# A two-branch decoder layer: the up product with tokens on the partitions, two of eight K-pairs by seven products

## The chip, the cores and the metric

The kernel runs on one core of one Trainium2 chip. The metric is the device time of one execution in microseconds (us). An interval or a verdict comes from several runs of both kernels on the same chip.

## What is computed

One decoder layer over 256 tokens of width 2048, in float32. An attention branch and an mLSTM branch fill the first part and end in a gated sum and an output projection. The second part is a feed-forward block, and the change is about this block:

```python
h2 = rmsnorm(x, norm2_g[l])
u = causal_dwconv(jnp.einsum('bsd,df->bsf', h2, w_up[l]), conv_w[l], conv_b[l])
u_gate, u_val = u[..., :D_FF], u[..., D_FF:]
x = x + jnp.einsum('bsf,fd->bsd', jax.nn.silu(u_gate) * u_val, w_down[l])
```

`w_up` is 2048 x 11264 and `w_down` 5632 x 2048. The convolution has three taps per channel and runs over the tokens: out[t] = w0 u[t-2] + w1 u[t-1] + w2 u[t] + b. So it wants the channels on the partitions and the tokens along the free dimension.

## The kernel before, in words

**Products in two parts.** Every operand is split into a high part (rounded to the float32r type) and a low part (the rest), and a product is three matmuls: low x high, high x high, high x low. For weights, ScalarE writes the high part `wh` (L159) and VectorE the low part `wl` (L160), piece by piece; a piece is 1024 columns wide. There are three buffers each of `wh` and `wl`, so the split runs at most two pieces ahead of TensorE. Weight chunks (1 MB, two pieces) come by SyncE's queue into three buffers `raw` (L122). `next_sub` (L165) hands TensorE its next piece and writes the split of the pieces after it into the program.

**Two forms of product.** With the tokens on the partitions (`block_b`, L233, and `s_block`, L267), 128 tokens are the stationary operand and 512 weight columns move: a 256 x 256 x 1024 piece of work, called a K-pair here (two K-tiles of 128, two token tiles, two column halves), takes 8 products, 24 matmuls of 512 columns. With the channels on the partitions (`block_a`, L260) the weights are stationary and the activations move: per K-tile one matmul of 512 columns (`wh` against the high and the low activation side by side) and one of 256 (`wl` against the high one).

**Seven products.** In `s_block` a pattern says for each K-pair whether it is done plainly ("p") or by seven products instead of eight ("S"), that is 21 matmuls instead of 24. For an "S" pair the weights need sums: the chunk gives four pieces, "b" (1024 columns), "b21" (512), "t13" (1024) and "t24" (1024). VectorE makes the sums (L144, L151, L154) besides the low parts, and the sum tile for "t24" is finished by L154, which is written with "t13". The activations need sums too (`put_sums`, L204). Such patterns stand in the gate projections, the output projection and the last product (Y_PAIRS, 8 of 22 pairs). TensorE and the vector engines each work through their own list in a fixed order that the compiler's scheduler sets.

**The up product before.** 88 blocks of 128 channels, gate and value in turn (`block_a`, called at L919), 16 K-tiles each. `up_evac` (L897) then adds the two halves of the PSUM tile (ScalarE L350, VectorE L351), multiplies by the row norm (`rb`, VectorE L900), and convolves (ScalarE L903, two VectorE instructions L905). Silu is on ScalarE (L923), the product with the value on VectorE (L926, into `gv`). Every second pair `put_pair` (L200) splits the result into the operand of the last product (`ghl`), and for the 8 "S" pairs of the last product `put_sums` writes sums that go out to DRAM (`s_dram`, L933) and come back after the up product (`s_ops`, L943). The normalisation is applied after the product, so `h2` is the plain sum stream times the gain, transposed (`transposed`, L848).

**Buffers.** A pool "a8" has 15 tiles of 8 KB per partition; the eleven `ghl` tiles and the four `h2` tiles fill it during the up product. Scratch has four 2 KB tiles.

**Elsewhere.** At the start, the squares of x for the first norm are taken on ScalarE from the transposed x and added up on GpSimd (`add_square`, L429). Before the gate projections, `normalised` (L602) loads the transposed x a second time by GpSimd's queue (L600, `hv`), scales it on VectorE (L607) and splits it into `hN`.

Of the kernel before, what the change touches and what calls it, by code (L numbers as in the profile page):

```python
# [17 lines left out]
P = 128  # L18
# [19 lines left out]
WO_PAIRS = "pSpSpppp"  # L38
Y_PAIRS = "ppp" + "Sp" * 7 + "S" + "pppp"
N_S = Y_PAIRS.count("S")  # L40

C_G1, C_G2, C_QG, C_KG, C_MG, C_CONV = 0, 16, 32, 33, 34, 42
CST = C_CONV + 2 * NF * 4


@with_exitstack  # L50
def trunk(ctx: ExitStack, tc: tile.TileContext, a):
# [19 lines left out]
    def scratch(name, shape, tag="w2k", bufs=4):  # L71
        return work.tile(shape, F32, tag=tag, bufs=bufs, name=name)
# [10 lines left out]
    def add_chunk(ap, n, pieces=("whole", "whole")):  # L83

        subs_of.extend((len(chunks), i, kind) for i, kind in enumerate(pieces))
        chunks.append((ap, n, ap.tensor.name))
# [19 lines left out]
    n = len(subs_of)  # L106
# [4 lines left out]
    raws, subs, s_tiles, last_of = {}, {}, {"of": None}, {}  # L111
    n_chunk = len(chunks)

    def load_chunk(i, part=None):
# [3 lines left out]
        src, n, _ = chunks[i]  # L118
# [5 lines left out]
    def split_sub(j):  # L124
# [142 lines left out]
    def s_block(name, pairs, s_ops, pattern, pools, dst, add=True, per_piece=0):  # L267
# [22 lines left out]
        for m, kind in enumerate(pattern):  # L290
# [18 lines left out]
            left -= 1  # L309
            if first:  # L310
                ps = {i: pools[1](f"{name}p{i}") for i in (1, 5, 7, 6)}
            s1, s2, s3, s4 = s_ops[m]
            w = piece()
# [46 lines left out]
    hT, _ = operand("hT")  # L360
# [64 lines left out]
    sq = const.tile([P, S], F32, name="sq")  # L425
# [3 lines left out]
    def add_square(x, first):  # L429

        if first:
            nc.scalar.activation(sq, x, AF.Square)
            return
        t = scratch("t2", [P, S], tag="u1k", bufs=5)
        nc.scalar.activation(t, x, AF.Square)
        nc.gpsimd.tensor_tensor(sq, sq, t, ALU.add)

    def norm(r):

        ps = aux_tile("ps_norm")  # L440
        for tok in range(2):
            mm(ps[:, tok : tok + 1], sq[:, tok * P : (tok + 1) * P], ones[:, :1], True, True)
        v = small("v", [P, 2], 1)
# [595 lines left out]
```

## Time and profile before

| what | value |
|---|---|
| median of 3 runs | 1399.7 us (1393.97 to 1401.78) |
| the profiled execution's own time | 1392.95 us |
| its span, first to last instruction | 1391.2 us |
| granted TensorE clock, mean | 0.999 |
| TensorE busy | 1378.4 us of the span |
| VectorE busy | 1056.4 us |
| ScalarE busy | 762.1 us |
| GpSimd busy | 49.7 us |
| matmuls of the up product | 1408 of 512 columns, 1408 of 256 |

How to read the profile: its page gives the busy time of each engine, the span in 40 slices, and the chain of work that ended last, followed back from the last instruction. PE is TensorE (PEld its weight loads), DVE VectorE, ACT ScalarE, POOL GpSimd, SP SyncE. Matmuls overlap in the pipeline, so the duration of one is longer than the distance from one start to the next; it is this distance that adds up to the time of a stage. The timeline shows it: start, length, instruction, and in brackets the idle time before it with what ended it. The same holds for VectorE: two independent instructions in a row overlap a little. L numbers are lines of the kernel before; rows of the changed kernel's order have that kernel's own lines (there the low part of a weight piece is L173, the sums L157, L164 and L167).

### The profile page before, as it was taken

The numbers are of one execution on the slowest core, as the hardware profiler recorded it, in microseconds if no ns is written. First come the engines' busy times: TensorE is split into PE (matmuls) and PEld (weight loads), VectorE is DVE, ScalarE is ACT, GpSimd is POOL, SyncE is SP. The second block draws the span as 40 slices with busy tenths as digits, with TensorE's granted clock in tenths as the row PEclk, the third lists the DMA queues.
The fourth block names the chain that finished last, engine by engine and source line by source line (L and its number), as shares of the span: only waits on it lengthen the run. The fifth ranks groups of instructions, "written<-read, shape, count | busy, mean of one in ns | idle before, by whom it ended". The sixth has DMA issues, their size and how long they took to land.

```text
span 1391.2 us, 18429 instructions
## 1 busy us (share of the span) xinstructions
PE 1378.4 (99%) x6956; PEld 1165.0 (84%) x6956; DVE 1056.4 (76%) x1493; ACT 762.1 (55%) x1086; POOL 49.7 (4%) x84
## 2 busy tenths in 40 slices
PE   8999999999999999999999999999999999999998
PEld 8978788888788888887888888888888888878877
DVE  7565566556888867777888888888888887886886
ACT  6645454444655544454755565656565554653553
POOL 6001100000000000000000000000000000000000
PEclk9999999999999999999999999999999999999999
DMA  7645564443555566465555556555555657657553
GB/s 253 213 180 182 197 227 156 168 161 122 181 193 221 191 229 220 160 229 217 186 191 201 194 195 207 191 199 199 208 203 182 231 201 266 220 185 270 205 188 121
DMA packets 43128, 276.25 MB, mean 199 GB/s; under 512 B 4960, under 2 KB 4976, under 8 KB 12192
## 3 DMA queue, kind: packets, MB, share of 16 engines
q1 hardware_dynamic: 39168, 260.20, 52.6%
q0 software_dynamic: 3728, 14.87, 3.0%
q8 instruction: 54, 0.88, 0.3%
q14 instruction: 34, 0.28, 0.1%
q10 hardware_dynamic: 144, 0.02, 0.0%
HBM read 267.73 MB, written 7.34 MB: 198 GB/s over the span
## 4 chain that ended last, share of the span: by engine, by line
PE 96%; DVE 2%; DMA 1%; ACT 0%; issue 0%; POOL 0%; ACTq 0%; DVEq 0%
PE up L220 35%; PE y0q L220 7%; PE y1q L220 7%; PE p L220 6%; PE mog L220 3%; PE fq L220 3%; PE mv L220 3%; PE fk L220 3%; PE wo0q L220 3%; PE wo1q L220 3%; PE g1q L220 2%; PE g3q L220 2%; PE g2q L220 2%; PE g0q L220 2%; PE fv L220 2%; PE y0p L220 2%
## 5 line engine op out<-in xcount | busy, mean ns | idle before, releaser
L159 ACT ACTIVATE wh<-raw 128x1024 fp32r<-128x1024 f32 (+2 forms) x496 | 505.8, 1021 | 473.9 <-PE up L220 120.3
L160 DVE TENSOR_TENSOR wl<-raw,wh 128x1024 fp32r<-128x1024 f32 (+2 forms) x496 | 580.3, 1182 | 200.4 <-ACT wh L159 198.2
L220 PE MATMUL up<-h,wh 128*128 128x512 f32 x1408 | 488.6, 391 | 0.0
L220 PE MATMUL up<-h,wl 128*128 128x256 f32 x1408 | 394.0, 280 | 0.0
L220 PEld LDWEIGHTS up<-h,wh 128*128 128x128 f32 x1408 | 263.2, 187 | 58.0 <-DVE h L189 0.2
L220 PEld LDWEIGHTS up<-h,wl 128*128 128x128 f32 x1408 | 266.1, 189 | 0.1
L160 DVE TENSOR_TENSOR wl<-sums,wh 128x1024 fp32r<-128x1024 f32 x58 | 70.9, 1223 | 46.6 <-ACT wh L159 46.6
L159 ACT ACTIVATE wh<-sums 128x1024 fp32r<-128x1024 f32 x58 | 61.5, 1060 | 67.1 <-PE y0q L220 19.4
L905 DVE SCALAR_TENSOR_TENSOR t<-u,cst,t 128x256 f32<-128x256 f32 x176 | 84.8, 482 | 3.8 <-ACT t L903 0.7
L220 PE MATMUL p<-wh,am 128*128 128x512 f32 x256 | 79.4, 391 | 0.0
L220 PE MATMUL y1q<-wh,ghl 128*128 128x512 f32 x256 | 78.1, 390 | 0.0
L220 PE MATMUL y0q<-wh,ghl 128*128 128x512 f32 x256 | 78.0, 390 | 0.0
L220 PEld LDWEIGHTS y1q<-wh,ghl 128*128 128x128 f32 x256 | 48.1, 188 | 10.1
L220 PEld LDWEIGHTS y0q<-wh,ghl 128*128 128x128 f32 x256 | 48.0, 188 | 10.1
L220 PEld LDWEIGHTS p<-wh,am 128*128 128x128 f32 x256 | 47.6, 188 | 9.7
L903 ACT ACTIVATE t<-u,cst 128x256 f32<-128x256 f32 x88 | 52.0, 591 | 1.8 <-DVE u L900 1.6
L220 PE MATMUL p<-wl,am 128*128 128x512 f32 x128 | 49.9, 390 | 0.0
L220 PE MATMUL y0q<-wl,ghl 128*128 128x512 f32 x128 | 48.9, 391 | 0.0
L220 PE MATMUL y1q<-wl,ghl 128*128 128x512 f32 x128 | 48.8, 390 | 0.0
L220 PE MATMUL mog<-wh,hT 128*128 128x348 f32 (+1 forms) x192 | 43.5, 337 | 2.4 <-ACT wh L159 1.9
L220 PE MATMUL g0q<-wh,hN 128*128 128x512 f32 x128 | 41.5, 404 | 0.0
L220 PE MATMUL mv<-wh,hT 128*128 128x512 f32 x128 | 40.2, 395 | 0.0
(372 smaller groups left out, 2032.0 us busy)
## 6 DMA issues: line engine op xcount, KB each, us to landing
raw<-in_w_up SPq DMA_DIRECT2D x88, 1024.0 KB, 4.9
raw<-in_w_dn SPq DMA_DIRECT2D x44, 1024.0 KB, 4.8
raw<-in_w_g SPq DMA_DIRECT2D x32, 1024.0 KB, 4.9
raw<-in_w_fox SPq DMA_DIRECT2D x24, 1024.0 KB, 4.8
raw<-in_w_p SPq DMA_DIRECT2D x16, 1024.0 KB, 4.9
raw<-in_w_out SPq DMA_DIRECT2D x16, 1024.0 KB, 4.9
raw<-in_w_mqk SPq DMA_DIRECT2D x8, 1024.0 KB, 4.8
raw<-in_w_mv SPq DMA_DIRECT2D x8, 1024.0 KB, 4.8
```

The lines of the kernel that those rows point to most:

```text
L159: nc.scalar.activation(wh[:, :n], src, AF.Copy)
L160: nc.vector.tensor_tensor(wl[:, :n], src, wh[:, :n].bitcast(F32), ALU.subtract)
L220: nc.tensor.matmul(out, lhsT, rhs, start=start, stop=stop)
L903: nc.scalar.activation(t, u[:, 2:], AF.Identity, scale=w[2], bias=w[3])
L905: nc.vector.scalar_tensor_tensor(out=t, in0=u[:, i : i + S], scalar=w[i], in1=t, op0=ALU.mult, op1=ALU.add)
```

## The change

The up product is done by `s_block`, tokens on the partitions, in 11 blocks of 1024 columns (512 gate, 512 value channels), each of eight K-pairs with the pattern "ppSpSppp". Its result `c` is token-major. VectorE adds the plain part to the seven-product part (four instructions of 512), ScalarE scales by a per-token factor `rho`. Then, during the next block, `as_columns` transposes it back on TensorE (four transposes of 128 columns for each of 44 channel groups), ScalarE copies it out of PSUM, and `convolved` does the convolution, Silu and the splits as before. A list of tasks says where: four empty tasks, then one transpose group, and so on, two tasks per weight piece, so that all of it falls into the first eight pieces of the twenty of a block. The row norm becomes: `x2` is scaled by `rs`, the norm of its first half, before it is transposed, and `rho` corrects to the full norm. The order of the K-pairs in the last product is rotated by six; the six pairs 0 to 5 are written to DRAM (`g_dram`) and read back (`gback`) before it, and the sums' scratch moves from the "mv" tile to the 2 KB scratch.

At the start the squares are taken from x in token-major form (`xt`, two loads of 1 MB by GpSimd's queue), eight ScalarE instructions of 512 with their own accumulator, and GpSimd's sums go. `normalised` rebuilds the operand from the split one already in SBUF (`whole`, one add, one multiply, one split) instead of loading x again.

The core of the diff:

```diff
+UP_PAIRS = "ppSpSppp"
+N_OUT = 6
+Y_ORDER = list(range(N_OUT, NF // 2)) + list(range(N_OUT))
...
-    add_b(a["w_up"], 512)
-    subs_of[n + 1], subs_of[n + 2] = subs_of[n + 2], subs_of[n + 1]
+    add_pairs(a["w_up"], [UP_PAIRS] * (NF // 4))
...
-        add_square(xT[k], k == 0)
+        if k == 2:
+            for tok in range(2):
+                nc.gpsimd.dma_start(xt[tok], a["x"][tok * P : (tok + 1) * P, :])
+        if k >= KD // 2:
+            tok, q = divmod(k - KD // 2, 4)
+            add_squares(ss1[:, tok, q : q + 1], xt[tok][:, q * 512 : (q + 1) * 512])
...
+    def whole(pair):
+        v = scratch("gv", [P, 2, S])
+        nc.vector.tensor_tensor(
+            v, pair[:, :, 0, :].bitcast(F32), pair[:, :, 1, :].bitcast(F32), ALU.add
+        )
+        return v
     def normalised(m):
-        load_x(m + 1)
-        v = hv.pop(m)
...
+        v = whole(hT_pairs[m])
+        nc.vector.tensor_tensor(v, v, rb.unsqueeze(1).to_broadcast([P, 2, S]), ALU.mult)
         put_pair(hN_pairs[m], v.rearrange("p k s -> p (k s)"))
...
+    def as_columns(j, c):
+        ps, at = (aux_tile if j // 4 % 2 == 0 else acc_tile)(f"ps_u{j}"), j % 4 * P
+        for h in range(2):
+            for tok in range(2):
+                nc.tensor.transpose(
+                    ps[:, h * S + tok * P : h * S + (tok + 1) * P],
+                    c[:, tok, h * 512 + at : h * 512 + at + P], ident,
+                )
+        us[j] = work.tile([P, 2, S], F32, tag="u2k", bufs=2, name=f"u{j}")
+        nc.scalar.activation(us[j].rearrange("p h s -> p (h s)"), ps, AF.Copy)
+    def convolved(j):
+        u, out = us.pop(j), []
+        for i in range(2):
...
+            nc.scalar.activation(t, u[:, i, :], AF.Identity, scale=w[2], bias=w[3])
+            for q in (1, 0):
+                d = 2 - q
+                nc.vector.scalar_tensor_tensor(
+                    out=t[:, d:], in0=u[:, i, : S - d], scalar=w[q], in1=t[:, d:], op0=ALU.mult,
+                    op1=ALU.add,
+                )
...
+        nc.vector.tensor_tensor(gv[:, (j % 2) * S : (j % 2 + 1) * S], sg, out[1], ALU.mult)
...
+            put_sums(gv, se, False)
...
+        put_pair(g_pairs[m], gv)
+        if m < N_OUT:
+            nc.gpsimd.dma_start(
+                g_dram[:, m], g_pairs[m].rearrange("p k l s -> p (k l s)")
+            )
...
+    for b in range(NF // 4):
+        pools = (aux_tile, acc_tile) if b % 2 == 0 else (acc_tile, aux_tile)
+        c = a8(f"c{b}", [2, 1024])
...
+        q = s_block(f"up{b}", h2_pairs, up_ops, UP_PAIRS, pools, dst, False, 2)
+        run_tasks(len(tasks))
+        for h in range(2):
+            for tok in range(2):
+                v = dst(tok, h)
+                nc.vector.tensor_tensor(v, v, q[tok][h], ALU.add)
+                nc.scalar.activation(v, v, AF.Copy, scale=rho[:, tok : tok + 1])
...
+        tasks.extend(nop * 4 + [ts[0]] + nop + [ts[1], es[0], ts[2], ts[3]] + nop + [es[1]])
+        tasks.extend(nop + [es[2]] + nop + [es[3]])
```

Where instructions move, first place: VectorE in the middle of the up product. Before, this is what stands there over two channel blocks (`wl` a low part, `sum` and `u` the result of a block, `t` the convolution, `gv` gate times value):

```order
L160 TENSOR_TENSOR wl_6609<-raw_6500,wh_6608 128x1024
L905 SCALAR_TENSOR_TENSOR t<-u_5538,cst,t 128x256 x2
L926 TENSOR_TENSOR gv<-sg,t 128x256
L160 TENSOR_TENSOR wl_6629<-raw_6553,wh_6628 128x1024
L351 TENSOR_TENSOR sum<-sum,up_6552 128x256
L900 TENSOR_TENSOR u_5536<-sum,rb 128x256
L160 TENSOR_TENSOR wl_6663<-raw_6553,wh_6662 128x1024
```

In the changed kernel this stands in the fifth block, from the plain pair between the two "S" pairs (chunk `raw_7105`) to the second piece but one of the second "S" pair (`raw_7167`):

```order
L173 TENSOR_TENSOR wl_7220<-raw_7105,wh_7219 128x1024
L953 SCALAR_TENSOR_TENSOR t<-u_7179,cst,t 128x255 x2
L953 SCALAR_TENSOR_TENSOR t<-u_7179,cst,t 128x254 x2
L173 TENSOR_TENSOR wl_7242<-raw_7105,wh_7241 128x1024
L964 TENSOR_TENSOR gv<-sg,t 128x256
L953 SCALAR_TENSOR_TENSOR t<-u_7186,cst,t 128x255 x2
L953 SCALAR_TENSOR_TENSOR t<-u_7186,cst,t 128x254 x2
L173 TENSOR_TENSOR wl_7268<-raw_7167,wh_7267 128x1024
L164 TENSOR_TENSOR sums<-raw_7167,sums 128x512
L199 TENSOR_TENSOR ghl_7213<-gv,ghl_7213 128x2x256
L167 TENSOR_TENSOR sums<-raw_7167,sums 128x512
L173 TENSOR_TENSOR wl_7304<-sums,wh_7303 128x1024
```

The convolution's instructions, which were spread evenly between the low parts, stand in a cluster, and the sums of the "S" pairs stand behind them.

Second place: TensorE at the same second "S" pair of the changed kernel (`up4p` and `up4q` are its PSUM tiles, `h` and `us` its activations; before, this stage is only `up` matmuls of 512 and 256 columns in turn):

```order
L233 MATMUL up4p_7188<-wh_7267,h_4789 128x512 x2
L233 MATMUL up4q_7068<-wh_7267,us 128x512 x2
L233 MATMUL up4q_7067<-wh_7284,h_4789 128x512
L233 MATMUL up4p_7188<-wl_7268,h_4789 128x512
L233 MATMUL up4q_7068<-wl_7268,us 128x512
L233 MATMUL up4q_7067<-wh_7284,h_4789 128x512
L233 MATMUL up4p_7189<-wh_7303,h_4789 128x512 x2
L233 MATMUL up4p_7190<-wh_7303,us 128x512
L233 MATMUL up4q_7067<-wl_7285,h_4789 128x512
L233 MATMUL up4p_7190<-wh_7303,us 128x512
L233 MATMUL up4p_7191<-wh_7313,us 128x512
```

The first matmul on `wh_7313` (the high part of "t24", which is made from the sum of L167) is the fourteenth of the 21 of this pair.

Third place: GpSimd at the start. Before (`sel` a mask, `sq` the sum of squares, `rows` and `cst` constants):

```order
L404 AFFINE_SELECT sel<-sel 96x1024
L436 TENSOR_TENSOR sq<-sq,t_269 128x256
L478 DMA rows<-in_rows 128x16
L436 TENSOR_TENSOR sq<-sq,t_290 128x256
L479 DMA cst<-in_cst 128x352
L436 TENSOR_TENSOR sq<-sq,t_311 128x256
```

After:

```order
L490 DMA rows<-in_rows 128x16
L417 AFFINE_SELECT sel<-sel 96x1024
L491 DMA cst<-in_cst 128x352
L417 AFFINE_SELECT sel<-sel 96x1024
L486 DMA xt_163<-in_x 128x2048
L486 DMA xt_164<-in_x 128x2048
```

The additions are gone, and the two loads of x stand behind the masks and the constants.

More of the change, by code (lines that the diff above doesn't have):

```diff
@@ L1 @@
-from contextlib import ExitStack, nullcontext
+from contextlib import ExitStack
 import numpy as np
@@ L359, in trunk @@
     xT = [xts[k // 8][:, k % 8] for k in range(KD)]
-    hT, _ = operand("hT")
+    hT, hT_pairs = operand("hT")
     def load_first(i):
@@ L422, in rsqrt_mean, with add_squares, norm @@
         nc.gpsimd.tensor_tensor(out, tmp, mhalf[:, : out.shape[1]], ALU.pow)
-    sq = const.tile([P, S], F32, name="sq")
     rb = const.tile([P, S], F32, name="rb")
     r1, r2 = const.tile([P, 2], F32, name="r1"), const.tile([P, 2], F32, name="r2")
[L429 to L443, printed above, removed]
-        rsqrt_mean(r, ps[:, :2], D, v)
+    def add_squares(ss, x):
+        nc.scalar.activation(junk_tile(512), x, AF.Square, accum_out=ss)
+    def norm(r, ss, n):
+        t, v = small("ss", [P, 2], 1), small("v", [P, 2], 1)
+        nc.vector.tensor_reduce(t, ss, AX.X, ALU.add)
+        rsqrt_mean(r, t, n, v)
     def as_rows(r):
@@ L616, in gate_sums @@
             g_ops["tile"] = a8(f"gs{i}", [2, 2, 512], F32R)
-        t, v = g_ops["tile"][:, i % 2], scratch("gv", [P, 2, S])
-        hi, lo = (hN_pairs[m][:, :, l, :].bitcast(F32) for l in range(2))
-        nc.vector.tensor_tensor(v, hi, lo, ALU.add)
+        t, v = g_ops["tile"][:, i % 2], whole(hN_pairs[m])
         put_sums(v.rearrange("p k s -> p (k s)"), (t[:, 0], t[:, 1]), True)
@@ L880, in trunk @@
             nc.gpsimd.dma_start(xs[:, tok, c], x2[tok][:, c])
-        tasks.extend([lambda k=k: transposed(k) for k in range(8 * b, 8 * b + 8, 2)])
+        tasks.extend([lambda m=m: transposed(m) for m in range(4 * b, 4 * b + 4)])
     def norm2():
-        ss, v = small("ss", [P, 2], 1), small("v", [P, 2], 1)
-        nc.vector.tensor_reduce(ss, ss2, AX.X, ALU.add)
-        rsqrt_mean(r2, ss, D, v)
-    g_tiles, g_pairs = operand("ghl", NF)
+        t = small("rinv", [P, 2], 1)
+        norm(r2, ss2, D)
@@ L946, in trunk @@
-    for i, m in enumerate(m for m, kind in enumerate(Y_PAIRS) if kind == "S"):
-        g = g_pairs[m]
-        y_ops[m] = [(g[:, 0, 0, P:], g[:, 0, 1, P:])] + [
-            (blocks[6 * i + c], blocks[6 * i + 3 + c]) for c in range(3)
+        blocks.extend(t[:, q * P : (q + 1) * P] for q in range(16))
+    n_sums = N_S * 6 // 16
+    for i in range(n_sums - 1):
+        load_sums(i)
+    tasks.append(lambda: load_sums(n_sums - 1))
+    s_pos = [pos for pos, kind in enumerate(Y_PAIRS) if kind == "S"]
@@ L950, in trunk, with sums_of @@
+    def sums_of(pos):
+        g, i = g_pairs[Y_ORDER[pos]], 6 * s_pos.index(pos)
+        return [(g[:, 0, 0, P:], g[:, 0, 1, P:])] + [
+            (blocks[i + c], blocks[i + 3 + c]) for c in range(3)
         ]
+    y_pairs, y_ops = Lazy(lambda pos: g_pairs[Y_ORDER[pos]]), Lazy(sums_of)
     for b in range(2):
```

200 lines of the change are left out of this document (108 added, 92 removed).

## The prediction

> **What bounds the kernel now.** I read the page first: busy times, the slices, the chain of waits.
>
> ```profile
> PE 1378.4 (99%) x6956; PEld 1165.0 (84%) x6956; DVE 1056.4 (76%) x1493; ACT 762.1 (55%) x1086; POOL 49.7 (4%) x84
> PE   8999999999999999999999999999999999999998
> DVE  7565566556888867777888888888888887886886
> PE 96%; DVE 2%; DMA 1%; ACT 0%; issue 0%; POOL 0%; ACTq 0%; DVEq 0%
> ```
>
> TensorE is busy throughout and carries 96% of the chain; VectorE is second. Next, the busy time by stage (up product, then the first half of the last product): start and end; length, then PE, PEld, DVE, ACT, POOL busy.
>
> ```profile
> 667.00:1155.00 488.00, 488.00 (x2816) 430.11 (x2815) 401.87 (x643) 288.89 (x433) 7.34 (x13) 1.00 0.57 200
> 1155.00:1271.00 116.00, 115.99 (x507) 93.42 (x506) 94.03 (x102) 60.93 (x65) 0.00 (x0) 1.00 0.62 226
> ```
>
> In the up product TensorE never stops and VectorE is busy for 82% (401.87 of 488); in the last product, which has seven-product pairs already, for 81% (94.03 of 116). ScalarE has room. So the time of this stage is a count of matmuls as long as VectorE keeps up, and VectorE has 18% to spare. The chain in order of time gives the distance between matmuls:
>
> ```profile
> 662.96 3.49 PE ps_h L853 x32
> 678.39 477.02 PE up L220 x2752
> 1248.99 22.26 PE y0q L220 x98
> ```
>
> 477.02/2752 is 173.3 ns, or 346.7 ns for a pair of one 512-column and one 256-column matmul. Token-major, 22.26/98 is 227 ns for 512 columns. A 128-column transpose takes 3.49/32 = 109 ns.
>
> **The change, TensorE.** Out: 1408 pairs of 346.7 ns, 488.1 us. In: 11 blocks of 6 x 24 + 2 x 21 = 186 matmuls, 2046 x 227 ns = 464.4 us, and 44 x 4 transposes of 109 ns, 19.2 us. Together 483.6, so TensorE gains **4.5 us**. From the two rows a matmul costs some 13 ns beside its columns (346.7 = 227 + 120, while half of 227 is 113.5), and the change issues 770 fewer matmuls; that is most of what it saves before the transposes. The Trainium skill (TensorE: Matmul & The Clock Gate, section Back-to-back issue gap) has N/2.4 + 2.5 ns, 216 for 512 columns and 109 for 256. By that estimate the swap saves 16 us instead of 24, and after the transposes it would cost 3 us; the trace has 227 where the page has 216, and I go by the trace.
>
> **The change, VectorE.** Durations first (the groups by shape: busy time, mean ns of one), then starts, since instructions overlap:
>
> ```profile
> L160 DVE TENSOR_TENSOR wl<-raw,wh 128x1024 fp32r<-128x1024 f32 x443 | 536.1, 1223 | 190.3 <-ACT wh L159 188.3 <-PE ps_s L220 1.6
> L159 ACT ACTIVATE wh<-raw 128x1024 fp32r<-128x1024 f32 x443 | 468.9, 1059 | 418.8 <-PE up L220 120.3 <-issue 83.5 <-PE p L220 47.1
> L159 ACT ACTIVATE wh<-raw 128x512 fp32r<-128x512 f32 x29 | 18.4, 633 | 41.7 <-PE y1q L220 13.9 <-PE y0q L220 12.9 <-PE g3q L220 3.8
> L903 ACT ACTIVATE t<-u,cst 128x256 f32<-128x256 f32 x88 | 52.0, 591 | 1.8 <-DVE u L900 1.6
> ```
>
> ```profile
> 163.00 1.68 DVE L607 SCALAR_TENSOR_TENSOR hv<-hv,cst,rb 128x256 f32<-128x256 f32 x4 [2.40 <-DMA hv<-in_xT]
> ...
> 799.87 1.00 DVE L905 SCALAR_TENSOR_TENSOR t<-u,cst,t 128x256 f32<-128x256 f32 x2
> ...
> 808.25 0.29 DVE L215 TENSOR_TENSOR sv<-gv 128x128 f32<-128x128 f32 x1
> 808.46 0.69 DVE L186 TENSOR_TENSOR ghl<-gv,ghl 128x512 fp32r<-128x512 f32 x1
> 809.06 0.29 DVE L216 TENSOR_TENSOR sv<-gv,sv 128x128 f32<-128x128 f32 x1
> ...
> 809.71 0.43 DVE L900 TENSOR_TENSOR u<-sum,rb 128x256 f32<-128x256 f32 x1
> 810.06 1.22 DVE L160 TENSOR_TENSOR wl<-raw,wh 128x1024 fp32r<-128x1024 f32 x1
> 811.19 0.55 DVE L186 TENSOR_TENSOR se<-sv,se 128x384 fp32r<-128x384 f32 x1
> 811.66 0.48 DVE L905 SCALAR_TENSOR_TENSOR t<-u,cst,t 128x256 f32<-128x256 f32 x1
> ```
>
> Start to start: 1.135 us for 1024 columns (810.06 to 811.19), 0.60 for 512, 0.47 for 384, 0.35 for a 256-column add or multiply, 0.21 for 128. A convolution step is 0.40 (four in 1.68, the last one's own 0.48 taken off) or 0.52 where it waits for the step before (two in 1.00).
>
> One block: 20 of 1024 (12 plain low parts; per S pair three low parts and one sum) is 22.7. Sixteen of 512 (two sums and one low part per S pair; 4 to join the seven products; 4 to add the plain part; 2 operand splits) is 9.6. Sixteen convolution steps are 6.6, four gate products 1.4, and `put_sums` (four of 128, one of 384, 1.3) in 8 of 11 blocks. That makes **40.3 us, or 41.6 with `put_sums`**, against 42.2 + 1.7 = 43.9 of TensorE. VectorE goes from 82% to 92 to 95%. It would still fit, were it spread evenly.
>
> It is not. The task list puts the convolution into the first eight of the twenty pieces, and the split may run only two pieces ahead. How little room there is at an S pair, the last product shows today:
>
> ```profile
> 1290.88 1.22 DVE L160 TENSOR_TENSOR wl<-sums,wh 128x1024 fp32r<-128x1024 f32 x1
> 1292.02 3.49 DVE L160 TENSOR_TENSOR wl<-raw,wh 128x1024 fp32r<-128x1024 f32 x3
> ...
> 1298.83 1.23 DVE L160 TENSOR_TENSOR wl<-sums,wh 128x1024 fp32r<-128x1024 f32 x1 [1.51 <-ACT wh L159]
> ```
>
> ```profile
> 1291.29 1.07 PE L220 MATMUL y1q<-wh,ghl 128*128 128x512 f32 x4
> 1292.20 0.46 PE L220 MATMUL y1p<-wl,s_ops 128*128 128x512 f32 x1
> ```
>
> The low part of "t24" ends at 1292.10 and TensorE takes it at 1292.20; VectorE's whole reserve is the 1.5 us idle once per pair of pairs. So I keep a ledger of one block, with t = 0 where TensorE starts it. Without a stall TensorE ends the two plain pairs, with four transpose groups of 0.44 between, at 12.65, the S pair at 17.4, the plain pair at 22.84, and wants the high part of the second "t24", the fourteenth matmul of that pair, at 22.84 + 13 x 0.227 = 25.8. That high part needs VectorE's sum (the last L167 of the order quoted above). From the low part of the first "b" to that sum stand seven of 1024 (7.95), six of 512 (3.6), sixteen steps (6.6) and four gate products (1.4), 19.6 us. It can't begin before 6.5: its buffer comes free when piece 2 is done (5.45), then ScalarE needs 1.06. So the sum is ready at 26.1 at the earliest, its high part 1.06 later at 27.1, and TensorE stands 1.3 us. Followed step by step, VectorE also waits for ScalarE some 1.3 us on the way: for the high part of the first "b21" (its buffer is free only at 8.6), for the second group's copy and tap (about 0.6 each), and for the high part of the first "t13". That makes **2.7 us a block**. In blocks with `put_sums` its four sums stand before the same sum: **3.6 us**. In the last four pairs VectorE catches up, so every block starts anew. Ten blocks carry a convolution, seven of them `put_sums`: 3 x 2.7 + 7 x 3.6 = **33 us**, at least 3 x 1.3 + 7 x 2.2 = 19. I take 33, since the waits follow from the same rows.
>
> The first block has no convolution but the second half of `h2` (12 steps, two `put_sums`, about 9 us in the same place): 1.5. Its start trades 32 transposes ahead of it for 16 ahead and 16 within, and a wait of 0.3 for the first low part. The last convolution falls into the last product behind six plain pieces; the same ledger there gives 0.7 + 0.75 + 0.3 + 1.0 = 2.8 at its first two S pairs. Costing nothing: ScalarE's copies and scalings (some 34 us of a block's 44, by durations like those above), the weights' DMA (same bytes), as long as ScalarE isn't the last.
>
> **The change, elsewhere.** Before the gates TensorE waits once for a low part, behind VectorE's wait for the second load of x:
>
> ```profile
> 171.96 0.88 DVE L607 SCALAR_TENSOR_TENSOR hv<-hv,cst,rb 128x256 f32<-128x256 f32 x2 [2.36 <-DMA hv<-in_xT]
> 174.03 0.50 PE L220 MATMUL fv<-wl,hT 128*128 128x512 f32 x1 [2.15 <-DVE wl L160]
> ```
>
> That load goes: at most -2.2, but `whole` gives VectorE 1.8 us a pair instead of 1.4, so 0 is the other end; -1.5. At the start:
>
> ```profile
> 13.67 0.71 POOL L478 DMA_DIRECT2D rows<-in_rows  x1
> 16.93 1.29 ACT L188 ACTIVATE hT<-xT,cst 128x256 fp32r<-128x256 f32 x3
> 18.25 0.91 PE L220 MATMUL mog<-wh,hT 128*128 128x348 f32 x4 [0.45 <-DVE hT L189]
> x<-in_x POOLq DMA_DIRECT2D x2, 1024.0 KB, 5.7
> s_ops<-s_dram POOLq DMA_DIRECT2D x3, 1024.0 KB, 9.9
> ```
>
> Two loads of 1 MB are issued about when `rows` is now, less the additions ahead of it (some 11), and land 5.7 us later or more; ScalarE's squares wait for them with `hT` of the next K-tiles behind (16.93), on which TensorE waits already. Between -0.5 and +3; 0.8.
>
> **Sum.** -4.5 + 33.3 + 1.5 + 0.3 + 2.8 - 1.5 + 0.8 = +32.7. The profiled execution's own time is 1392.95 (its span 1391.2 and 1.75 around it), so 1425.7 by its clock; it lies 6.75 below the median 1399.7, and beside the median that is **1432**. With all low ends: -4.5 + 19 + 0 + 0 + 1 - 2.2 - 0.5 = +13, 1413; with 3 at the start and 5 us more waiting, 1440.
>
> **Rivals.** (1) VectorE keeps up: its waits overlap with what I count and the stalls go. Then the matmul count decides: -4.5 - 1.5 + 0.8, 1394.5. It holds if 19.6 us in the ledger are under 18.3. For it: 92 to 95% still fits on the whole. Against it: the 0.1 us of 1292.10 to 1292.20. 0.14, of which 0.05 under 1392.7, where the start and the g stages gain a little too. (2) VectorE doesn't overlap instructions at these places: each counts with its duration, 0.08 more. 33 instructions of the ledger are 2.6 us more, 26 over ten blocks and the last product's 2.6: 1461. The row of three in 3.49 (not 3.67) speaks against it; 0.04. The Trainium skill (VectorE: DVE Perf Modes, section The DRAIN you can't avoid) says that the next instruction doesn't start until the pipe is empty, which would be this case; here starts are 1.135 apart at a duration of 1.22. (3) The spilled pairs hold up the last product: six loads of 512 KB stand before `s_ops` in GpSimd's queue. The first S pair comes 18 us into it and `s_ops` lands in 9.9, so it decides if they start over 8 us late; if all six wait for the up product's end at some 2.9 each, 17 us, they are 9 late: 1441. Against it: two pool tiles are free before. 0.10.
>
> **How the numbers follow.** The forecast has 0.72, of which 0.02 lies below 1406.7; 0.5% (7 us) is about what a measurement of this kernel can tell. Faster: 0.05 from (1). Same: 0.09 from (1) and 0.02. Slower: 0.70 + 0.04 + 0.10 = 0.84. The range leaves out (1), (2) and those 0.02, 0.20 in all, and takes in the low and high ends and (3) with some room: 1407 to 1446.
>
> **What would show it.** In the up product TensorE's idle time should be 30 us and more, in gaps of 2 to 4 us once a block, ended by `wh` or `wl` of sums at the second S pair, with VectorE busy for over 85% and at work without a break before each gap. Low parts start 1.135 apart. If those gaps are missing and the stage is some 484 us, the ledger is wrong; if they sit at the boundary of blocks, it is the evacuation (`c`, `rho`, the transposes) and not the cluster.

## The result, and the profile after

The changed kernel takes 1435.6 us (median of 4 runs, 1433.6 to 1437.8) against 1400.0 us for the kernel before (4 runs, 1394.0 to 1401.8). The ratio is 1.0263, with a 95% interval of 1.0227 to 1.0298: slower. The profiled execution of the changed kernel took 1436.96 us with a span of 1435.2, so the two profiled spans lie 44.0 us apart while the medians lie 35.6 apart: the kernel before comes at 1391 to 1395 or at 1400 to 1404 from one execution to the next, at the same granted clock, and its profiled execution was one of the short ones, so stages are compared below by the profiled executions and totals by ratios. Lines below are the changed kernel's: the low part of a weight piece is L173, its high part L172, the sums L157, L164 and L167, a convolution step L953, a matmul L233.

The page of the changed kernel, the busy times and VectorE's row of the slices:

```profile
PE 1392.1 (97%) x6356; PEld 1139.1 (79%) x6356; DVE 1120.2 (78%) x1526; ACT 828.9 (58%) x1152; POOL 44.0 (3%) x81
...
DVE  5555766557888767878888889888988897987786
```

TensorE does 600 instructions less (6956 before) and yet has 43 us of idle time in its span, where it had 13. Next, the busy times of stretches: five blocks of the up product, the first half of the last product, and in a second view the up product as a whole. After the colon of a row come its length, then PE, PEld, DVE, ACT and POOL busy, the granted clock, the share of DMA and GB/s.

```profile
669.00:714.20 45.20, 44.74 (x202) 36.30 (x203) 37.50 (x56) 29.06 (x44) 1.03 (x2) 1.00 0.55 196
714.20:764.90 50.70, 47.88 (x203) 38.10 (x202) 42.40 (x62) 33.24 (x46) 2.17 (x4) 0.93 0.58 194
...
857.90:904.40 46.50, 44.66 (x203) 36.22 (x202) 41.42 (x57) 31.23 (x44) 0.00 (x0) 1.00 0.52 181
904.40:953.40 49.00, 46.62 (x204) 37.49 (x203) 42.72 (x62) 31.93 (x45) 1.06 (x2) 0.97 0.53 180
953.40:1000.70 47.30, 44.95 (x204) 36.27 (x203) 42.49 (x62) 31.69 (x45) 1.06 (x2) 1.00 0.54 186
...
1192.80:1314.10 121.30, 118.37 (x522) 94.89 (x522) 102.31 (x123) 69.08 (x83) 1.64 (x3) 1.00 0.63 228
```

```profile
669.00:1192.80 523.80, 500.79 (x2222) 404.06 (x2223) 459.15 (x650) 346.76 (x482) 16.65 (x31) 0.98 0.56 196
```

The up product takes 523.8 us; it took 488.8. VectorE is busy for 90% of a block's time (42.49 of 47.30), where it was 82%. Three kinds of block show: 46.5 us (57 VectorE instructions), 47.3 us (62, the five of `put_sums` more), and longer ones in which the clock column is under 1.00.

Where a block loses its time is in the timeline. TensorE in the fifth block, which starts at 857.90, around the second S pair (`up4p` and `up4q` are its PSUM tiles, `us` the activations' sums):

```profile
875.43 0.50 PE L233 MATMUL up4p<-wl,us 128*128 128x512 f32 x1 [0.28 <-DVE wl L173]
...
884.21 0.40 PE L233 MATMUL up4p<-wh,us 128*128 128x512 f32 x1
886.16 0.50 PE L233 MATMUL up4p<-wh,us 128*128 128x512 f32 x1 [1.55 <-ACT wh L172]
```

And VectorE over the same stretch, with ScalarE's instruction that ends the gap:

```profile
875.29 1.22 DVE L173 TENSOR_TENSOR wl<-raw,wh 128x1024 fp32r<-128x1024 f32 x1
876.42 1.66 DVE L953 SCALAR_TENSOR_TENSOR t<-u,cst,t 128x255 f32<-128x255 f32 x4
878.00 1.22 DVE L173 TENSOR_TENSOR wl<-raw,wh 128x1024 fp32r<-128x1024 f32 x1
879.14 0.42 DVE L964 TENSOR_TENSOR gv<-sg,t 128x256 f32<-128x256 f32 x1
879.47 1.67 DVE L953 SCALAR_TENSOR_TENSOR t<-u,cst,t 128x255 f32<-128x255 f32 x4
881.05 1.22 DVE L173 TENSOR_TENSOR wl<-raw,wh 128x1024 fp32r<-128x1024 f32 x1
882.19 0.43 DVE L964 TENSOR_TENSOR gv<-sg,t 128x256 f32<-128x256 f32 x1
882.52 0.69 DVE L164 TENSOR_TENSOR sums<-raw,sums 128x512 f32<-128x512 f32 x1
883.12 0.69 DVE L173 TENSOR_TENSOR wl<-raw,wh 128x512 fp32r<-128x512 f32 x1
883.73 0.69 DVE L199 TENSOR_TENSOR ghl<-gv,ghl 128x512 fp32r<-128x512 f32 x1
884.33 0.69 DVE L167 TENSOR_TENSOR sums<-raw,sums 128x512 f32<-128x512 f32 x1
...
887.29 3.49 DVE L173 TENSOR_TENSOR wl<-raw,wh 128x1024 fp32r<-128x1024 f32 x3
```

```profile
885.05 1.06 ACT L172 ACTIVATE wh<-sums 128x1024 fp32r<-128x1024 f32 x1 [1.29 <-DVE sums L167]
```

None of VectorE's rows has a bracket: it does not wait here. Every instruction starts before the one ahead has ended, and the sum of L167 is done only at 885.0, 27.1 us into the block. ScalarE stood 1.29 us for it, and TensorE stood 1.55 us for ScalarE's high part, at the fourteenth matmul of the pair. The smaller gap, 0.28 us for a low part, is at the end of the first S pair.

In the blocks with `put_sums` the second S pair has two gaps, mostly 0.9 us for a low part and 1.2 us for the high part. The longer blocks have something behind these gaps. TensorE in the sixth block:

```profile
931.82 0.50 PE L233 MATMUL up5q<-wl,h 128*128 128x512 f32 x1 [0.91 <-DVE wl L173]
933.51 0.97 PE L233 MATMUL up5p<-wh,us 128*128 128x512 f32 x2 [1.19 <-ACT wh L172]
934.28 0.63 PE L233 MATMUL up5q<-wh,h 128*128 128x512 f32 x1
934.71 0.63 PE L233 MATMUL up5p<-wl,h 128*128 128x512 f32 x1
935.14 0.63 PE L233 MATMUL up5p<-wl,us 128*128 128x512 f32 x1
935.56 1.49 PE L233 MATMUL up5q<-wh,h 128*128 128x512 f32 x3
936.84 0.58 PE L233 MATMUL up5p<-wl,us 128*128 128x512 f32 x1
937.26 0.39 PE L233 MATMUL up5q<-wl,h 128*128 128x512 f32 x1
```

From 933.5 to 937.3 matmuls start up to 0.43 us apart instead of 0.227, and the granted clock of this stretch is 0.55: the array runs at about half its clock for some 3.7 us, in which 9 matmuls start instead of 16 or 17, and 1.7 us are lost. That is why this block takes 49.0 us and its neighbour with the same gaps, but a clock of 1.00, 47.3.

At the start, TensorE's wait for a K-tile and the stretch around it:

```profile
21.19 0.91 PE L233 MATMUL mog<-wh,hT 128*128 128x348 f32 x4 [1.87 <-DVE hT L202]
```

```profile
10.00:20.00 10.00, 9.32 (x42) 9.04 (x42) 4.85 (x8) 3.31 (x5) 0.00 (x0) 0.72 1.02 392
```

The DMA engines move 392 GB/s there (260 before) and the granted clock is 0.72 (1.00 before); the stage ends at 61.7 us instead of 57.5.

| stage (difference of the two profiled executions) | forecast, us | measured, us |
|---|---|---|
| start, to the first matmul of `fq` | +0.8 | +4.2 |
| from there to the first gate matmul (second load of x) | -1.5 | -2.1 |
| gates to the up product's start (16 transposes less ahead of it) | -1.4 | +0.4 |
| up product: matmuls and transposes | -4.5 | -0.1 |
| up product: stalls in ten blocks | +33.3 | +27.1 |
| up product: the clock behind the stalls | not counted | +6.8 |
| up product: first block | +1.5 | +1.2 |
| up product in all | +30.3 | +35.0 |
| first half of the last product (1.7 of transposes, 2.8 of waits) | +4.5 | +5.5 |
| second half and end | 0 | +1.0 |
| sum | +32.7 | +44.0 |

The measured values of matmuls, stalls and clock in the up product can't be read from these two executions alone. They are worked out behind the experiments, from the run with both repairs and the run with matmuls that add zero.

### The profile page after: what moved, and what is told of

It is laid out like the page before. It is cut to its first block, busy times and chain, and to the rows that moved or that the text cites. A ratio compares the mean times of both kernels' runs of the same rounds, so it can differ in the third digit from the quotient of the medians.

```text
span 1435.2 us, 17408 instructions
## 1 busy us (share of the span) xinstructions
PE 1392.1 (97%) x6356; PEld 1139.1 (79%) x6356; DVE 1120.2 (78%) x1526; ACT 828.9 (58%) x1152; POOL 44.0 (3%) x81
## 5 line engine op out<-in xcount | busy, mean ns | idle before, releaser
L172 ACT ACTIVATE wh<-raw 128x1024 fp32r<-128x1024 f32 (+2 forms) x496 | 491.9, 999 | 402.5 <-PE p L233 47.1
L173 DVE TENSOR_TENSOR wl<-raw,wh 128x1024 fp32r<-128x1024 f32 (+2 forms) x496 | 563.5, 1150 | 186.5 <-ACT wh L172 183.7
L173 DVE TENSOR_TENSOR wl<-sums,wh 128x1024 fp32r<-128x1024 f32 x102 | 124.0, 1222 | 48.6 <-ACT wh L172 48.1
L172 ACT ACTIVATE wh<-sums 128x1024 fp32r<-128x1024 f32 x102 | 107.7, 1057 | 75.1 <-PE y1q L233 19.1
L953 DVE SCALAR_TENSOR_TENSOR t<-u,cst,t 128x255 f32<-128x255 f32 (+1 forms) x176 | 76.6, 480 | 4.4 <-ACT t L950 3.7
L233 PE MATMUL p<-wh,am 128*128 128x512 f32 x256 | 79.5, 391 | 0.0
L157 DVE TENSOR_TENSOR sums<-raw 128x1024 f32<-128x1024 f32 x51 | 62.4, 1224 | 5.8 <-DMA raw<-in_w_dn 3.4
L233 PEld LDWEIGHTS p<-wh,am 128*128 128x128 f32 x256 | 47.6, 188 | 9.7
L233 PE MATMUL y0q<-wh,ghl 128*128 128x512 f32 x172 | 52.6, 392 | 0.0
L233 PE MATMUL y1q<-wh,ghl 128*128 128x512 f32 x172 | 52.1, 390 | 0.0
L233 PE MATMUL p<-wl,am 128*128 128x512 f32 x128 | 49.9, 390 | 0.0
L950 ACT ACTIVATE t<-u,cst 128x256 f32<-128x256 f32 x88 | 48.3, 594 | 0.7
L233 PE MATMUL mog<-wh,hT 128*128 128x348 f32 (+1 forms) x192 | 43.9, 340 | 4.1 <-DVE hT L202 4.1
L996 ACT ACTIVATE c<-c,rho 128x512 f32<-128x512 f32 x44 | 31.6, 720 | 25.4 <-DVE c L995 25.4
L233 PE MATMUL g0q<-wh,hN 128*128 128x512 f32 x128 | 41.3, 401 | 0.0
L233 PE MATMUL mv<-wh,hT 128*128 128x512 f32 x128 | 40.3, 396 | 0.0
L233 PE MATMUL fq<-wh,hT 128*128 128x512 f32 x128 | 40.0, 394 | 0.0
L233 PE MATMUL fk<-wh,hT 128*128 128x512 f32 x128 | 39.8, 392 | 0.0
L233 PE MATMUL fv<-wh,hT 128*128 128x512 f32 x128 | 39.6, 391 | 0.0
L233 PEld LDWEIGHTS mog<-wh,hT 128*128 128x128 f32 x192 | 35.0, 203 | 5.3 <-ACT wh L172 3.1
L233 PEld LDWEIGHTS y1q<-wh,ghl 128*128 128x128 f32 x172 | 32.3, 188 | 6.9
L233 PEld LDWEIGHTS y0q<-wh,ghl 128*128 128x128 f32 x172 | 32.1, 188 | 6.7
```

Source lines behind the costliest of these rows:

```text
L157: nc.vector.tensor_tensor(sums[:, :1024].rearrange("p (i c) -> p i c", i=2), raw[:, :512].unsqueeze(1).to_broadcast([P, 2, 512]), src.rear ...
L172: nc.scalar.activation(wh[:, :n], src, AF.Copy)
L173: nc.vector.tensor_tensor(wl[:, :n], src, wh[:, :n].bitcast(F32), ALU.subtract)
L233: nc.tensor.matmul(out, lhsT, rhs, start=start, stop=stop)
L950: nc.scalar.activation(t, u[:, i, :], AF.Identity, scale=w[2], bias=w[3])
L953: nc.vector.scalar_tensor_tensor(out=t[:, d:], in0=u[:, i, : S - d], scalar=w[q], in1=t[:, d:], op0=ALU.mult, op1=ALU.add,)
```

## The experiments

Theory 1 is the prediction's: the convolution's VectorE work, clustered in the first eight weight pieces, stands ahead of the sums of the second S pair. Theory 2 is the way of the result out of PSUM (adding, scaling, transposing). Theory 3 is VectorE's load, wherever it stands. Ratios are to the kernel before on the same chip.

**The S pairs later.**

```diff
-UP_PAIRS = "ppSpSppp"
+UP_PAIRS = "ppppSpSp"
```

> The same work, with the two seven-product pairs moved to places 5 and 7 of the eight (pattern ppppSpSp), so that the convolution's VectorE instructions stand before the sums of the first of them only. Theory 1 (the cluster of the convolution stands ahead of the sums of the second S pair): the gaps of 2 us and more inside a block go, blocks last 44 to 45 us instead of 46.5 to 50.7, the up stage about 488 to 496 us, the whole 1400 to 1409 us. Theory 2 (the result's way out: adding, scaling and transposing c): nothing of that moves, so 1430 to 1437. Theory 3 (VectorE has too much to do in a block, 92 to 95 per cent, and waits come wherever it is placed): 1425 or more, with gaps at the new S pairs.

Measured: 1405.9 us, ratio 1.0046 (1.0015 to 1.0077). A block in the middle of the up product, and ten microseconds of the last product:

```profile
893.30:938.10 44.80, 44.80 (x204) 36.11 (x203) 42.08 (x62) 31.38 (x45) 1.06 (x2) 1.00 0.57 197
```

```profile
1182.00:1192.00 10.00, 7.54 (x19) 4.90 (x18) 9.96 (x19) 8.38 (x14) 0.00 (x0) 0.67 0.31 105
```

VectorE is as busy as before (42.08 us of the block, now 94%), and TensorE has no idle time: 44.8 us instead of 49.0. Theories 2 and 3 are out. The whole lies 7 us above the next run; in the profiled execution (1412.2, the longest of seven) 5.6 us of the difference are in the last product's first half, where the clock fell to 0.67 behind the last convolution's gaps.

**Half of the convolution behind the second S pair.** The pattern stays; only the list of tasks changes (the last block keeps its own).

```diff
-        tasks.extend(nop * 4 + [ts[0]] + nop + [ts[1], es[0], ts[2], ts[3]] + nop + [es[1]])
-        tasks.extend(nop + [es[2]] + nop + [es[3]])
+        tasks.extend(nop * 4 + [ts[0]] + nop + [ts[1], es[0]] + nop + [es[1]])
+        tasks.extend(nop * 22 + [ts[2]] + nop + [ts[3], es[2]] + nop + [es[3]])
```

> The same work and the same pattern; in blocks 1 to 10 the third and fourth transpose group of a block and their convolution are moved from the third to eighth weight piece to the seventeenth to nineteenth, behind the second S pair. Ahead of the sum of that pair stand eight convolution steps, two products and a split less, about 4.4 us by the rows of before (8 x 0.41, 2 x 0.35, 0.6). Theory 1: the stalls of 2.7 and 3.6 us and what the granted clock loses after them go in blocks 1 to 10: 1399 to 1408 us. Theory 2: 1430 to 1437, since as much is added, scaled and transposed. Theory 3: 1425 or more, with gaps somewhere else in the block.

Measured: 1398.7 us, just under the 1399 to 1408 that were expected; ratio 0.9993 (0.9973 to 1.0014), level with the kernel before. The fifth block and the eighth:

```profile
844.80:889.50 44.70, 44.70 (x204) 36.11 (x203) 41.29 (x57) 31.36 (x44) 0.00 (x0) 1.00 0.57 200
...
978.50:1022.80 44.30, 44.30 (x204) 36.21 (x203) 42.07 (x62) 31.67 (x45) 1.07 (x2) 1.00 0.58 199
```

The same instructions in another order, and the up product takes 489.8 us instead of 523.8: 34 us, nearly the whole loss of this stage, was the order on VectorE, with what the clock lost behind the stalls.

**One tap less.** This kernel leaves the tap two tokens back out of the convolution.

```diff
-            for q in (1, 0):
+            for q in (1,):
```

> One of the two VectorE taps of the convolution (the one two tokens back) is left out of the computation: eight instructions less in a block, 8 x 0.41 = 3.3 us, all of them ahead of the second S pair's sum; TensorE's work is the same. Theory 1: 2.7 us of stall in a block fall to 0 and 3.6 to 0.3, and the clock's loss behind them goes: 1396 to 1405 us. Theory 3 gives much the same here (VectorE at 85 instead of 93 per cent), so this run is against theory 2, by which the time stays at 1430 to 1437.

Measured: 1408.0 us, above the 1396 to 1405 that were expected; ratio 1.0047 (1.0032 to 1.0062). Blocks without `put_sums` fall to 44.6 us, but those with it only to 45.6, with a gap of 1.0 for ScalarE's `wh`:

```profile
938.20:983.80 45.60, 44.62 (x203) 36.33 (x202) 39.54 (x54) 31.70 (x45) 1.06 (x2) 1.00 0.57 193
```

```profile
951.14 1.22 DVE L173 TENSOR_TENSOR wl<-sums,wh 128x1024 fp32r<-128x1024 f32 x1 [0.85 <-PE ps_u L937]
...
963.68 0.68 DVE L167 TENSOR_TENSOR sums<-raw,sums 128x512 f32<-128x512 f32 x1
```

The sum ends at 26.2 us into the block where the full kernel's same block has 27.9: only 1.7 of the 3.3 us taken away arrive, since VectorE, now less behind, waits more for TensorE and ScalarE on its way (0.85 in the row above and 0.58 ahead of it, where the full kernel has none and 0.33). The mechanism holds; the expectation of 0.3 left over was too low, because a ledger that runs full turns into one that waits.

**No S pairs in the up product.**

```diff
-UP_PAIRS = "ppSpSppp"
+UP_PAIRS = "pppppppp"
...
-                nc.vector.tensor_tensor(v, v, q[tok][h], ALU.add)
-                nc.scalar.activation(v, v, AF.Copy, scale=rho[:, tok : tok + 1])
+                nc.scalar.activation(v, q[tok][h], AF.Copy, scale=rho[:, tok : tok + 1])
```

> The changed kernel with no seven-product pairs in the up product (pattern pppppppp; the result is scaled straight from PSUM). TensorE has 192 matmuls in a block instead of 186, 1.4 us more; VectorE loses the sums, the joins and two low parts of 512, some 9 us a block, and no sum stands behind the convolution any more. Theory 1 (the stall needs a sum of an S pair behind the cluster): no gaps, blocks of about 192 x 0.227 + 16 x 0.109 = 45.3 to 45.8 us, so the up stage is some 500 to 504 us against 523.8 with the pairs, and the whole 1410 to 1416 us: shorter without the saving than with it. Theory 2 (the result's way out): blocks of 47 us or more and 1430 or more, since the way out is the same.

Measured: 1409.0 us, 1 us under the expected range; ratio 1.0115 (1.0093 to 1.0136).

```profile
848.30:893.70 45.40, 45.40 (x209) 37.65 (x208) 28.73 (x38) 27.67 (x39) 0.00 (x0) 1.00 0.53 186
```

192 x 0.227 + 16 x 0.109 is 45.3; the block takes 45.4. The cluster stands where it stood, nothing behind it is waited for, and TensorE never stops. So the seven products, placed as the change places them, cost 1.5 per cent more than doing without them.

**Matmuls that add zero, in the gaps.**

The call `fill` writes `fills` such matmuls into the program; `fills` is 4 in the second to eleventh block.

```diff
...
+            fill(ps[6], fills if last else 0)
             prod(ps[5], s1, w, 0, first, last)
             prod(ps[7], s3, w, 1, first, last)
             w = piece()
+            fill(ps[6], fills if last else 0)
             prod(ps[6], s2, w, 0, first, last)
...
```

> The changed kernel with up to eight extra matmuls that add zero (bf16, 512 columns, no operand to wait for) at the second S pair of blocks 1 to 10, in the two gaps; they keep TensorE at work while it would stand there. Theory of the clock (in blocks 1, 5, 7 and 10 the gaps of 0.9 and 1.2 us let the granted clock fall to 0.93 to 0.97, and matmuls at half pace afterwards cost 3.4 us in the first and 1.5 in the others, some 8 in all): the granted clock is 1.00 in every block, the blocks last 46.5 to 47.3 us, and the whole is 4 to 8 us shorter than the changed kernel, 1428 to 1432 us. Rival (these blocks are longer because VectorE is later there, and the clock has no part): the time is that of the changed kernel or up to 8 us longer, where the extra matmuls of 0.22 us stand in the way.

Measured: 1432.9 us, ratio 1.0224 (1.0208 to 1.0240). The sixth block, and ten microseconds of the last product, where nothing was filled in:

```profile
900.20:947.50 47.30, 46.49 (x211) 36.86 (x210) 42.49 (x62) 31.69 (x45) 1.06 (x2) 1.00 0.54 187
```

```profile
1204.40:1214.40 10.00, 7.86 (x24) 5.54 (x25) 10.00 (x18) 7.49 (x12) 0.00 (x0) 0.83 0.28 105
```

All eleven blocks have a clock of 1.00, and the four long ones shrink from 50.7, 49.0, 48.8 and 48.7 to 48.3, 47.3, 47.3 and 47.5: 6.8 us. The work and the waits of the vector engines are as before, so these 6.8 us were the clock's. In the whole the medians lie only 2.7 us apart, where 4 to 8 were expected, and the intervals of the two ratios overlap; in the profiled execution the clock fell in the last product's gaps instead (its first half took 124.7 us, 3.4 more). So the loss is confirmed in the up product and not in the total, and where a drop falls differs from one execution to the next.

**The old start.** The changed kernel with the norm of before at the start: no loads of x there, sums on GpSimd.

```diff
...
-        if k == 2:
-            for tok in range(2):
-                nc.gpsimd.dma_start(xt[tok], a["x"][tok * P : (tok + 1) * P, :])
-        if k >= KD // 2:
-            tok, q = divmod(k - KD // 2, 4)
-            add_squares(ss1[:, tok, q : q + 1], xt[tok][:, q * 512 : (q + 1) * 512])
+        add_square(xT[k], k == 0)
...
```

> The changed kernel with the norm of before at the start: squares from the transposed x, added on GpSimd, and no loads of x by GpSimd's queue there. Theory of the start (those loads move 2 MB beside the weights, the K-tiles of hT come later, TensorE waits some 4 us for them and loses clock behind that): the first stage ends at 57 to 58.5 us instead of 61.7, and the whole is 2 to 4 us shorter than the changed kernel, 1431 to 1434. Rival (the wait comes from the order of ScalarE's and VectorE's work at the start, the squares among it, and not from the loads): it ends at 60 to 62, and the whole stays within 1 us of 1435.6.

Measured: 1428.8 us, ratio 1.0256 (1.0233 to 1.0279). The first stage ends at 56.9 us instead of 61.7:

```profile
10.00:20.00 10.00, 6.72 (x39) 5.94 (x38) 10.00 (x12) 6.04 (x14) 7.12 (x10) 1.00 0.93 329
```

4.8 us are gained at the start; the up product stays at 522.3. The total doesn't settle what this is worth. The median and the profiled span are 6.9 and 8.5 us shorter than the changed kernel's, but the ratio hardly moves (1.0256 against 1.0263, and the intervals overlap), since the kernel before has a median of 1392.9 on this chip and had 1400.0 beside the changed kernel. The stage does: the five runs ahead of this one have the start of the change untouched, and there it ends at 61.6, 59.3, 61.5, 60.6 and 61.1 us; with the old start it ends at 56.9 here and at 56.0 and 56.4 in the two runs below that have it too.

**The loads held back.** The changed kernel with its two loads issued only when the high part of the eleventh K-tile is there, and the squares behind the K-tiles.

```diff
+        if k == 10:
+            for tok in range(2):
+                nc.gpsimd.tensor_copy(xt[tok][:, :1], hT[k][:, 0, :1].bitcast(F32))
+                nc.gpsimd.dma_start(xt[tok], a["x"][tok * P : (tok + 1) * P, :])
...
+    tasks.extend([squares, lambda: norm(r1, ss1, D), lambda: as_rows(r1)])
```

> The changed kernel with its two loads of x at the start held back until the eleventh K-tile's high part is written, and the eight squares put behind the first stage's K-tiles. Nothing else moves. Theory of the loads (2 MB beside the first weights and K-tiles make hT late): the wait for hT near 20 us shrinks to under 0.5 us, the granted clock between 10 and 30 us is 0.95 or more, and the first stage ends at 57 to 58.5 us, near the 56.9 of the run with the start of before. Rival (GpSimd's masks in one unbroken row slow VectorE's first instructions, 3.60 us for two, and the rest follows from that): the wait in the first 10 us stays at 2 us and the stage ends at 60 us or later.

Measured: 1431.2 us, ratio 1.0279 (1.0264 to 1.0294, against a before of 1393.4). The stage ends at 59.3.

```profile
7.42 2.07 PE L233 MATMUL mog<-wh,hT 128*128 128x348 f32 x6 [2.81 <-DVE hT L202]
```

```profile
10.00:20.00 10.00, 10.00 (x51) 9.74 (x52) 6.55 (x11) 5.06 (x9) 0.00 (x0) 0.79 0.78 278
```

The wait for `hT` at 21 us is gone. All six executions with the loads in their place have it, at 20 to 21 us and 1.9 to 4.0 us long, so that wait came from the loads. (The edit also moves the squares, but in the changed kernel these begin only at 22.1, behind the wait. The runs with the old start, without such loads, have a shorter wait for `hT`, 1.2 to 1.5 us at 17 to 18 us, whose cause stays open.) What the wait costs is not shown: the stage ends 2.4 us earlier than in the changed kernel, but the run with half of the convolution later, with its loads not held back, ends it at the same time:

```profile
L233 PE MATMUL fq<-wh,hT x128: 387/389/501, 59.3 to 106.6; 128*128 128x512 f32 x128
```

The first wait, 2.8 us here, and a clock of 0.79 behind it stay, as the rival said, but 59.3 lies between what the theory (57 to 58.5) and the rival (60 or later) expected. Whether GpSimd's masks in one row cause the first wait is not settled: they coincide with VectorE's slow first instructions, but with the old start VectorE is slow too, a little later (3.25 us for two of these instructions at 8.24).

**Both repairs.** Half of the convolution later, and the old start.

> The two repairs together: half of the convolution behind the second S pair, and the start of before. If they add up: the time of the run with the half later, 1398.7, less 1.5 to 3: 1395.5 to 1397, which would be 3 to 4 us under the kernel before (ratio 0.997 to 0.998). If the start's gain is lost again in a later stage: 1398 to 1399, the same as before.

Measured: 1394.9 us (12 runs), ratio 1.0000 (0.998 to 1.002), where 0.997 to 0.998 was expected. The gains add up within the trace (up product 489.9, first stage to 56.0); against a before whose median was 1392.9 here, the kernel is level and not faster. The up product itself, with 0.5 us of idle time of TensorE, is 1.1 us longer than before's 488.8.

**The last product's first S pair one place later**, on top of both repairs.

```diff
-Y_PAIRS = "ppp" + "Sp" * 7 + "S" + "pppp"
+Y_PAIRS = "pppp" + "Sp" * 7 + "S" + "ppp"
...
-    for i in range(n_sums - 1):
+    for i in range(n_sums - 2):
...
-    tasks.append(lambda: load_sums(n_sums - 1))
+    tasks.extend([lambda i=i: load_sums(i) for i in range(n_sums - 2, n_sums)])
```

Besides the pattern, two of the three loads of sums are now issued within the last product, where it was one.

> As the two repairs together, and in the last product the first S pair stands fifth instead of fourth (pppp before it, ppp after the last), so that the last convolution has 5.45 us more before the first sums are wanted. Theory 1 (the last convolution's cluster stands ahead of these sums too: gaps of 1.7 us and more in the first 40 us of the last product): they go or shrink to under 0.5, 1.5 to 2.5 us less than the run without this, 1393 to 1395. Rival (the gaps come from the six pairs and the sums read back from DRAM): the gaps go to another place and the time is the same within 0.5 us.

Measured: 1397.4 us, ratio 1.0028 (1.0012 to 1.0044): 2.4 us longer, where 1.5 to 2.5 shorter was expected. The last product's first half did gain, 119.0 us instead of 119.9, with 1.4 us of waits left. But the pairs of the last product that need `put_sums` are now the even ones, so `put_sums` moves from the second half of the convolution to the first, ahead of the second S pair of the up product; the eighth block takes 44.7 with it where it took 44.3:

```profile
976.60:1021.30 44.70, 44.51 (x203) 36.11 (x202) 42.61 (x62) 31.73 (x45) 1.06 (x2) 1.00 0.58 197
```

That is theory 1 once more, in small: 1.3 us of VectorE work put ahead of the sum cost about 0.4 us a block in a kernel that had just enough room.

**The kernel before with `whole` alone.**

```diff
-        load_x(m + 1)
-        v = hv.pop(m)
...
+        v = scratch("gv", [P, 2, S])
+        hi, lo = (hT_pairs[m][:, :, l, :].bitcast(F32) for l in range(2))
+        nc.vector.tensor_tensor(v, hi, lo, ALU.add)
+        nc.vector.tensor_tensor(v, v, rb.unsqueeze(1).to_broadcast([P, 2, S]), ALU.mult)
```

> The kernel before with one part of the change alone: the normalised operand is rebuilt from the split one in SBUF (add, multiply, split) instead of a second load of x; its up product is untouched. Theory (the second load's late arrival is what TensorE waits 2.15 us for in the fv stage, and the extra add of 0.35 us a pair is hidden): that wait is gone, the stage from fv to the gates is 2 to 2.5 us shorter, and the whole is 2 to 4 us under before (ratio 0.997 to 0.9985). Rival (VectorE's extra 3 us of adds take the place of the wait): ratio 0.9995 to 1.001.

Measured: 1388.9 us against 1393.4, ratio 0.9982 (0.9968 to 0.9997). From the first matmul of `fv` to that of the gates:

```profile
L220 PE MATMUL fv<-wh,hT x128: 387/389/476, 149.8 to 193.8; 128*128 128x512 f32 x128
```

```profile
L220 PE MATMUL g0q<-wh,hN x128: 387/389/590, 298.5 to 356.0; 128*128 128x512 f32 x128
```

148.7 us, where the kernel before has 150.9 (150.7 to 301.6). The wait for the second load is gone and nothing takes its place. This one part of the change, without the rest, is 0.2 per cent faster than the kernel before, by an interval that ends just under 1.

## Why the prediction held, and where its steps did not

**The mechanism.** The ledger gave the sum ready at 27.4 us (26.1 and 1.3 of VectorE's own waits); the trace has 27.1. The wait sits at the fourteenth matmul, ended by the high part of the sums. Low parts start 1.135 us apart again (three in 3.49, the last one's 1.22 taken off), so the second rival, instructions that don't overlap, is out. That it is the order and not the load is shown by the run with half of the convolution later.

**The size of the stalls** came out smaller than the forecast. TensorE's idle time in the up product is 23.0 us (523.80 less 500.79), where the prediction wanted to see 30 and more. A gap costs a little more than its idle time: the start at 886.16 comes 1.95 us after the one at 884.21, 1.72 more than the usual 0.227, at an idle time of 1.55, since the matmul at 884.21 itself lasts 0.40. Counted from start to start, the fifth block loses 2.2 us and the seventh 3.0, against 2.7 and 3.6 in the forecast. In the fifth block the sum is 0.3 us earlier than the ledger has it, and without the smaller gap TensorE would want the high part 0.3 us later, at 26.1 instead of 25.8. For the whole stage, the changed kernel's 523.8 less the 489.9 of the run with both repairs is 33.9; less 6.8 for the clock that leaves 27.1 for stalls, against 33.3.

**What the step of the up product left out: the clock.** The prediction priced a gap at its length only. Four of the ten blocks took 48.7 to 50.7 us; in the run with zero matmuls in the gaps they take 47.3 to 48.3, which puts the clock's part at 6.8 us of the 35.0. The rows quoted in the prediction could not show it, since each has a clock of 1.00 and TensorE without a pause. The stalls were forecast 6.2 us too long and the clock's 6.8 us were missing: that the two nearly cancel is luck.

**The start** was put at "Between -0.5 and +3; 0.8", and was 4.2 in this execution, outside its own bounds; over the six executions with this start it was 1.8 to 4.2. The mechanism named there, ScalarE's squares waiting with `hT` behind them, is not what the trace shows: the squares begin at 22.1, after the wait:

```profile
22.13 0.61 ACT L443 ACTIVATE junk<-xt 128x512 bf16<-128x512 f32 x1
```

The trace has three things there: a wait that goes when the loads are held back (1.9 us), an earlier wait (2.2 us) and a clock of 0.72 between them. How the 4.2 us divide among them is not shown.

**The gates to the up product** were put at 0.3 beside 16 transposes less; measured is one of 1.8 for the first operands of the up product, in the list of TensorE's waits:

```profile
PE up0q L233 <- DVE h L202: 1.8, 1, 1.8
```

**The second load of x** was taken at -1.5 and the low end, -2.2, was right: the additional adds are hidden.

**TensorE's own 4.5 us** are not there in full. Almost without idle time (the run with both repairs) the up product is 1.1 us longer than before instead of 4.5 shorter. Of these 5.6 us the first block has 1.2; the others take 44.3 to 44.8 where 186 matmuls and 16 transposes give 43.96, while plain blocks take their 45.4. So an S pair saves 0.3 to 0.55 us and not 0.68. A part of what lengthens it can be seen: waits too short to count as idle time. In the fifth block of that run, at the first S pair, a matmul on the low part of a sum starts 0.39 us after the one before it (two start 0.227 apart from 855.21 on), just behind the low part, which VectorE writes from 854.54 to 855.77:

```profile
855.21 0.61 PE L233 MATMUL up4p<-wh,h 128*128 128x512 f32 x2
855.83 0.50 PE L233 MATMUL up4p<-wl,h 128*128 128x512 f32 x1
```

How much of the missing saving such waits make up is not worked out.

**The total** was off by 11 us in the traces (1425.7 forecast, 1436.96 measured) and by 3.6 beside the median, because before's profiled execution lies 7.0 us under its median and the changed kernel's 1.3 us above. Part of the closeness is therefore chance, beside the two errors of the up product that cancel; the direction and 27 of the 33 us of stalls are not.

**The rivals.** VectorE keeping up (1394.5) did not happen, and its price was too low: it is 5.2 us under the kernel before, while the kernel in which VectorE is given room, with the old start, is level with before (1.0000). That this run's median is 1394.9 is a coincidence, since before's median on that chip is 1392.9. Spilled pairs holding up the last product: no wait there is for `gback` or `s_ops`; its gaps are for `wh` and `wl` behind the last convolution, some 3 us in all.

## What to carry to other kernels

A share of busy time does not say whether an engine keeps up: follow what stands in its queue between the moment an operand can be begun and the moment it is wanted. If that is longer than the distance, move the work that nobody waits for behind it, before making anything cheaper; here this was worth 34 us, while leaving out half of the convolution's VectorE steps was worth 25 in the same stage. And add to the price of a gap what the clock does afterwards: here, in four of ten blocks, two gaps of 2 to 3 us together cost 1.2 to 2.4 us more.

## What the runs showed of the hardware

The granted clock fell to one half for about 3.7 us after two gaps of 0.91 and 1.19 us that lay 0.5 us apart, in some blocks and not in others with the same gaps (0.9 and 1.2 us), and in other blocks in other runs with the same up product: here the sixth, the eighth and the eleventh, with the old start the sixth and the ninth. The Trainium skill (TensorE: Matmul & The Clock Gate, section Part 1: The HAM clock gate) has the half clock after an idle window of some 3.4 us, and a window that runs freely. The length of the half-clock stretch and the changing place agree with a free window; the idle time needed does not: no gap within the up product was longer than 1.7 us, and 2.1 us of idle time in 2.6 were enough. At the start of the run with the old start four gaps of 4.2 us in all, spread over 12 us, left the clock at 1.00.
